# A Strassen-style float32 transformer block: where the first norm's diagonal tiles live, how fast the first FFN's queue drains, and how the projection groups are paired

## The chip, the cores and the metric

The kernel runs on one core of a Trainium2 chip. It is written for the core's engines directly: TensorE (PE in the profile) multiplies, PEld is its weight load, VectorE (DVE) and ScalarE (ACT) work element by element, and SyncE (SP) issues the DMA transfers. The metric is device time in microseconds (us) of one execution, the median over runs.

## The reference

One layer of a streaming encoder on x of shape (1, 1024, 1024), in float32:

```
h = x + 0.5 * SwiGLU_1(RMSNorm(x))                       # w_in 1024 x 5632, w_out 2816 x 1024
u = RMSNorm(h)
q, k, v, g_ret, p, gates = split(u @ w_in)               # 1024 columns each, gates 2048
q, k = rotary(q), rotary(k) / 16                         # 4 heads of 256
ret  = headnorm(retention(q, k, v)) * silu(g_ret)        # chunks of 64, decay per head
pool = (trailing means of p, windows 2/4/8/16, - p) @ pool_w * pool_scale
gate = sigmoid(gates + gate_bias)
h = h + (gate[0] * (ret @ w_ret_up) + gate[1] * (pool @ w_pool_up)) @ w_out
h = h + 0.5 * SwiGLU_2(RMSNorm(h))
return RMSNorm(h)
```

## The kernel before

Everything is float32, made on TensorE from two parts of each operand: a rounded high part, cast by ACT (line 161), and the rest, subtracted by DVE (line 162). A product of two such operands is three matmuls (lines 181 to 183). On top of that each group of 256 output channels by 1024 tokens is computed by a Strassen scheme of seven products (`strassen`): sums of weight blocks (S1 to S4, made by DVE at lines 484 to 501) against sums of input blocks. In a trace `q1a`, `q1b`, `q1e` are the PSUM banks of group q1, `q1ra` and `q1rb` its loaded weight rows, `q1S` a weight sum, `q1wS` and `q1wL` split weights of a sum or a loaded block, and `q1A`, `q1B` the group's two output tiles. An evacuation adds or copies PSUM into such a tile (lines 1200 and 1202 in the projections).

Two groups at a time are interleaved product by product (`pairs` in the projections, `pairs_of_both` in the FFNs), since they share operands; the last two products of a pair share work (`common`), in which the pair's banks `x` and `y` stand.

The order of the work is written in Python and each engine executes it in order. `Flow.run` walks the steps (one per product): it prepares a step's weights four steps ahead, emits the product, and then takes `flow.rate` items from the front of the queue `flow.back`. Into this queue go things that are not urgent: squares and norms, scalings by a norm's row, rotations, windows, gates and stores. `flow.until` (through `mix.rms()` or an operand) pulls items forward until what is asked for is there. All loads and stores go through the one queue of SP, in order (line 140). Tiles come from rings: `raw` and `tl` (128x1024, 4 buffers each; `tl` holds the loaded rows of x at the start), `t4` (128x1024, 9), `c2` (128x512, 8).

RMSNorm is not applied to the inputs. Each token's inverse root is spread over the partitions as a row (`spread`: diagonal tiles times ones on TensorE; n10b and n11b are the two halves for the first norm, n1rb is the row, n2rb that of the second), and outputs that need it are multiplied by that row. In the first FFN (`ffn_in`) a gate tile `ag` is scaled (line 777), put through Silu and multiplied with the up tile (`times`, line 783), and further operand blocks of the first norm (n1x, split into n1R) are made by DVE in the same queue.

The projections handle 24 groups of 256 channels in 12 pairs, in the sequence `order`, each by `project(kind, n)`:

- q and k (n = 0 to 3): not scaled. Groups with n < 3 are rotated here: `rotate` does six DVE operations a half (lines 1221 to 1230), twelve a group; the tables cos and sin are scaled by n2rb first (line 1182). Groups q3 and k3 are turned later, in the retention.
- p (n = 0 to 3): scaled by n2rb, then `window`: n + 1 doublings a half (line 1262) and a mean (lines 1269 to 1272).
- t (n = 0 to 7): the branch gates, scaled by n2rb, then four sigmoids on ACT (line 1249), each stored.
- g (n = 0 to 3): the retention's output gate, scaled, then Silu on ACT (line 1240).

A sigmoid and a Silu each need a table loaded on ACT (ACT_TABLE_LOAD). The scalings, rotations, windows and gates of a group go to the queue, and so run mostly beside the next pair's products.

Of the kernel before, what the change touches and what calls it, by code (L numbers as in the profile page):

```python
# [11 lines left out]
F32R = mybir.dt.float32r  # L12
# [5 lines left out]
P = 128  # L18
S = 1024
D = 1024  # L20
KT = D // P
H = S // 2
# [28 lines left out]
N_MV, N_T4, N_RAW, N_WT, N_TL, N_C2 = 28, 9, 4, 5, 4, 8  # L51
# [39 lines left out]
def block_kernel(ctx: ExitStack, tc, x, x_tok, x_two, vecs, f1_in, f1_out, w_in, w_v, pool_w, w_ret, w_pool, w_o,  # L91
# [8 lines left out]
    flow = Flow()  # L100

    cp = ctx.enter_context(tc.tile_pool(name="cp", bufs=1))
    sb = ctx.enter_context(tc.tile_pool(name="sb", bufs=1))
# [22 lines left out]
    def t4(name):  # L126
        return sb.tile([P, S], F32, tag="t4", bufs=N_T4, name=name)
# [4 lines left out]
    def bank(name):  # L132
        return ps.tile([P, H], F32, tag="ps", name=name)

    def sum_bank(name):

        return ps.tile([P, H], F32, tag="sum", bufs=N_SUM, name=name)
# [4 lines left out]
    def eights(name):  # L142

        return sb.tile([P, 32], F32, tag="ss", bufs=2, name=name)[:, :8]
# [4 lines left out]
    def half(t, j):  # L149
        return t[:, j * H : (j + 1) * H]  # L150
# [9 lines left out]
    def split(hi, lo, src):  # L160
        copy(hi, src)  # L161
        tt(lo, src, hi.bitcast(F32), SUB)  # L162
# [25 lines left out]
    def in_turns(x):  # L188

        return x.rearrange("p (o b a) -> p o a b", b=2, a=4)  # L190

    def in_row(x):
        return x.rearrange("p (o a b) -> p o a b", b=2, a=4)
# [24 lines left out]
    for n in range(N_SUM):  # L218
        b = sum_bank(f"set{n}")
# [7 lines left out]
    def inverse_root(sums, n, name, eps=None):  # L227

        m = sums.shape[-1]

        def st(k):
            return sb.tile([P, 8], F32, tag="st", bufs=10, name=f"{name}{k}")[:, :m]

        v, r0, r1, t = st("v"), st("r0"), st("r1"), st("t")
        for z, e in enumerate(eps or (EPS,)):
            at = slice(z * m // len(eps), (z + 1) * m // len(eps)) if eps else slice(0, m)
            nc.vector.tensor_scalar(v[:, at], sums[:, at], 1.0 / n, e, MUL, ADD)
        act(r0, v, AF.Sqrt)
        nc.vector.reciprocal(r1, r0)

        tt(t, r1, v, MUL)
        stt(t, t, -0.5, r1, MUL, MUL)
        r = sb.tile([P, 8], F32, tag="rt", bufs=3, name=f"{name}r")[:, :m]
        stt(r, t, 1.5, r1, ADD, MUL)
        return r

    def token_sums(ssq, tiles, name):

        sums = bank(f"{name}sum")
        for k, j in enumerate(tiles):  # L250
            mm(sums[:, k : k + 1], ssq[:, j * P : (j + 1) * P], ones[:, :1], start=k == 0, stop=True,
               skip_group_check=True)
        return sums[:, : len(tiles)]

    def spread(r, name):

        n = r.shape[-1]
        b = bank(f"{name}b")[:, : n * P]
        r2 = sb.tile([P, 2, 8], F32R, tag="r2", bufs=1, name=f"{name}r2")
        split(r2[:, 0, :n], r2[:, 1, :n], r)  # L260
        for z in range(2):
            dg = sb.tile([P, H], F32R, tag="c2", bufs=N_C2, name=f"{name}dg{z}")[:, : n * P]
            for j in range(n):
                at, by = dg[:, j * P : (j + 1) * P], r2[:, z, j : j + 1].bitcast(F32)
                if z:
                    nc.vector.tensor_scalar(at, ident, by, None, MUL)
                else:
                    act(at, ident, AF.Copy, scale=by)
            mm(b, ones_r, dg, start=not z, stop=bool(z))
        return b  # L270
# [26 lines left out]
    class Next(Norm):  # L297
# [139 lines left out]
                for i in range(4):  # L437
                    flow.add(lambda f=f, i=i: f(i))

        def stats(self, sums=None, between=()):  # L440
            def roots():
                t = sums if sums is not None else token_sums(self.ssq, range(8), self.name)
                self.r_tok = inverse_root(t, D, self.name)

            def row(q):
                if not q:
                    self.row = t4(f"{self.name}rb")
                to, b = half(self.row, q), spread(self.r_tok[:, 4 * q : 4 * q + 4], f"{self.name}{q}")
                if sums is not None:
                    to, b = in_row(to), in_turns(b)  # L450
                copy(to, b)
                if q:
                    self.rb = self.row

            n = max(0, len(between) - 3)
            flow.add(roots, *between[:n], lambda: row(0), *between[n:], lambda: row(1))
# [656 lines left out]
    first = Next("n1", V_FFN1)  # L1113
# [20 lines left out]
    x_sums = eights("x_sums")  # L1134

    def x_square(t):
        r = tl(f"xs{t}")
        load(r, x_tok[t])
        act(r, r, AF.Square, accum_out=x_sums[:, t : t + 1])

    for t in range(8):
        flow.add(lambda t=t: x_square(t))
    first.stats(x_sums)

    ops1 = spill("r", FH), spill("t", FH), spill("b", FH), spill("m", FH, H)
    h1, h2 = spill("h1", KT), spill("h2", KT)
# [8 lines left out]
    def fetch_rows(w, name):  # L1155
        for k in range(2):
            r = fetched[name, k] = wide(f"{name}ra{k}")
            load(r, w[k, :, :S])

    def ffn1():  # L1160
        for n, step in enumerate(ffn_in(first, f1_in, ops1, "a", lambda: fetch_rows(f1_out, "b"), lead)):
            flow.rate = 1
            yield step
        flow.rate = 2
        yield from ffn_out(first, ops1, ops_done["a"], f1_out, x_two, "b", mix.quarter, end1, fetched)
# [231 lines left out]
        yield from product("L22", "T4", "a", False, result(1, 0))  # L1397

    light = [("t", n) for n in range(8)] + [("g", n) for n in range(4)]
    turned = [(kind, n) for n in range(1, 4) for kind in "qk"]  # L1400
    heavy = [o for pair in zip([("p", n) for n in (1, 3, 2, 0)], turned) for o in pair] + turned[4:]
    order = [("q", 0), ("k", 0), *(o for pair in zip(heavy, light) for o in pair), *light[len(heavy) :]]

    def projections():
        yield from values()
# [472 lines left out]
    class Last(Norm):  # L1878


        tiles, rows, banks, sums = {}, {}, {}, {}
# [68 lines left out]
        def end(self, part):  # L1950
            if part != 3:
                return
            tokens = slice(H, S)
            at = {}

            def stats():
                r = inverse_root(token_sums(self.ssq, range(tokens.start // P, tokens.stop // P), "fin0"), D, "fin0")
                at["b"] = spread(r, "fin0")

            def scale(mt):  # L1960
                t = self.tiles[mt][:, tokens]
                stt(t, t, vec[:, V_FINAL + mt : V_FINAL + mt + 1], at["b"], MUL, MUL)
                load(out[mt, :, tokens], t)

            flow.add(stats, *(lambda mt=mt: scale(mt) for mt in range(KT)))
# [3 lines left out]
    def second():  # L1969
        for n, step in enumerate(ffn_in(ffn2, f2_in, ops2, "c", lambda: fetch_rows(f2_out, "d"))):  # L1970
            flow.rate = 1
            yield step
        flow.rate = 2
    flow.run(chain(ffn1(), projections(), retention(), merge(), second(),
                   ffn_out(ffn2, ops2, ops_done.setdefault("c", set()), f2_out, h2, "d", fin.quarter, fin.end, fetched, fin, f2_far)))
    flow.some(-1)
# [95 lines left out]
```

## Time and profile before

| | us |
|---|---|
| median of 3 runs | 2068.88 |
| the runs | 2070.76, 2068.88, 2068.75 |
| the profiled execution | 2069.82 |
| its span in the trace | 2068.0 |
| first FFN's first gate scaling starts | 84.58 |
| projections' first pair starts | 682.50 |
| retention starts | 1118.74 |

The profiled execution's time contains its span and 1.8 us around it. The granted clock of TensorE is full throughout. In a row of a trace the first number is the start in us from the span's start, the second the duration; `out<-in` are tile names without their buffer numbers; brackets give the engine's idle time before the row and what ended it. A matmul row of 128x512 starts 0.216 us after the one before when nothing is late, although its own duration reads 0.38: the rows overlap in the pipeline. So lost time on TensorE is read from the distances of starts.

### The profile page before, as it was taken

What the parts mean: (1) busy time and instruction counts of PE and PEld (TensorE: products, weight loads), DVE (VectorE), ACT (ScalarE), POOL (GpSimd) and SP (SyncE); (2) the same over time, 40 slices, a digit from 0 to 9 for tenths busy, and PEclk for the clock granted to TensorE, in tenths of its full rate; (3) what the DMA queues carried; (4) which work ended last, traced back from release to release, by engine and by line L of the source; (5) the groups of instructions that cost most, each with busy time, mean ns of one, the idle gap of its engine ahead of it and who ended that gap; (6) DMA issues with size and microseconds to landing.
All of it is one profiled execution on the core that took longest, in us unless ns stands there. A gap on an engine that the chain in (4) does not pass through costs nothing.

```text
span 2068.0 us, 29692 instructions
## 1 busy us (share of the span) xinstructions
PE 2045.2 (99%) x10672; PEld 1810.6 (88%) x10672; DVE 1835.5 (89%) x3262; ACT 1091.5 (53%) x2061; POOL 0.2 (0%) x4
## 2 busy tenths in 40 slices
PE   9999999999999999999999999999999999999998
PEld 7888999988888888888888999888789999998887
DVE  8799998997996798999778888999989989899897
ACT  8545444554653535454447753456645545455454
POOL 0000000000000000000000000000000000000000
PEclk9999999999999999999999999999999999999999
DMA  7232424585543333243336576724223242368642
GB/s 257 88 138 77 143 87 143 199 278 190 186 145 100 115 112 131 85 146 120 122 123 237 189 233 235 253 92 159 75 82 138 88 142 87 133 209 268 215 144 101
DMA packets 118819, 313.57 MB, mean 152 GB/s; under 512 B 13200, under 2 KB 17424, under 8 KB 118672
## 3 DMA queue, kind: packets, MB, share of 16 engines
q1 hardware_dynamic: 118096, 310.64, 44.3%
q8 instruction: 83, 1.36, 0.3%
q10 hardware_dynamic: 576, 1.05, 0.1%
q14 instruction: 64, 0.52, 0.1%
HBM read 220.93 MB, written 90.70 MB: 151 GB/s over the span
## 4 chain that ended last, share of the span: by engine, by line
PE 79%; DVE 14%; ACT 3%; issue 2%; DMA 1%; SPq 0%; ACTq 0%; DVEq 0%
PE a_b L181 2%; PE a_b L182 2%; PE a_b L183 2%; PE c_b L181 2%; PE c_b L182 2%; PE c_b L183 2%; PE a_e L181 2%; PE a_e L183 2%; PE a_e L182 2%; PE c_e L183 2%; PE c_e L182 2%; PE c_e L181 2%; PE a_a L182 1%; PE a_a L181 1%; PE a_a L183 1%
## 5 line engine op out<-in xcount | busy, mean ns | idle before, releaser
L182 PE MATMUL c_b<-n3T,c_wS 128*128 128x512 f32 x176 | 66.8, 380 | 0.0
L181 PE MATMUL c_b<-n3T,c_wS 128*128 128x512 f32 x176 | 66.5, 380 | 0.2 <-ACT n3T L161 0.2
L183 PE MATMUL c_b<-n3T,c_wS 128*128 128x512 f32 x176 | 66.7, 379 | 0.0
L181 PE MATMUL a_b<-n1T,a_wS 128*128 128x512 f32 x168 | 63.7, 379 | 0.0
L182 PE MATMUL a_b<-n1T,a_wS 128*128 128x512 f32 x168 | 63.7, 379 | 0.0
L183 PE MATMUL a_b<-n1T,a_wS 128*128 128x512 f32 x168 | 63.7, 379 | 0.0
L181 PE MATMUL a_a<-n1R,a_wL 128*128 128x512 f32 x120 | 45.5, 379 | 0.0
L183 PE MATMUL a_a<-n1R,a_wL 128*128 128x512 f32 x120 | 45.5, 379 | 0.0
L182 PE MATMUL a_a<-n1R,a_wL 128*128 128x512 f32 x120 | 45.5, 379 | 0.0
L182 PE MATMUL c_a<-n3R,c_wL 128*128 128x512 f32 x112 | 42.7, 381 | 1.1 <-DVE n3R L166 1.1
L181 PE MATMUL c_a<-n3R,c_wL 128*128 128x512 f32 x112 | 42.6, 380 | 0.8 <-ACT c_b L521 0.8
L183 PE MATMUL c_a<-n3R,c_wL 128*128 128x512 f32 x112 | 42.5, 379 | 0.0
L181 PEld LDWEIGHTS c_b<-n3T,c_wS 128*128 128x128 f32 x176 | 33.2, 189 | 5.1 <-ACT n3T L161 0.6
L182 PEld LDWEIGHTS c_b<-n3T,c_wS 128*128 128x128 f32 x176 | 33.3, 189 | 4.8 <-DVE n3T L162 0.3
L183 PEld LDWEIGHTS c_b<-n3T,c_wS 128*128 128x128 f32 x176 | 33.3, 189 | 4.7
L183 PEld LDWEIGHTS a_b<-n1T,a_wS 128*128 128x128 f32 x168 | 31.8, 189 | 4.5
L182 PEld LDWEIGHTS a_b<-n1T,a_wS 128*128 128x128 f32 x168 | 31.8, 189 | 4.4
L181 PEld LDWEIGHTS a_b<-n1T,a_wS 128*128 128x128 f32 x168 | 31.8, 189 | 4.3
L162 DVE TENSOR_TENSOR a_wS<-a_S,a_wS 128x512 fp32r<-128x512 f32 x45 | 30.6, 682 | 5.3 <-ACT a_wS L161 5.2
L161 ACT CAST c_wS<-c_S 128x512 fp32r<-128x512 f32 x46 | 27.8, 622 | 11.8 <-DVE c_S L484 7.4
L182 PE MATMUL c_e<-n3T,c_wL 128*128 128x512 f32 x88 | 33.5, 380 | 0.1
L181 PE MATMUL c_e<-n3T,c_wS 128*128 128x512 f32 x88 | 33.5, 380 | 0.0
(3159 smaller groups left out, 8001.9 us busy)
## 6 DMA issues: line engine op xcount, KB each, us to landing
c_ra<-in_f_in SPq DMA_DIRECT2D x22, 512.0 KB, 3.7
c_rb<-in_f_in SPq DMA_DIRECT2D x22, 512.0 KB, 3.7
a_ra<-in_f_in SPq DMA_DIRECT2D x21, 512.0 KB, 3.8
a_rb<-in_f_in SPq DMA_DIRECT2D x21, 512.0 KB, 3.8
t<-au SPq DMA_DIRECT2D x11, 512.0 KB, 3.0
b<-ag SPq DMA_DIRECT2D x11, 512.0 KB, 3.8
r<-au SPq DMA_DIRECT2D x11, 512.0 KB, 3.7
bra<-in_f_out SPq DMA_DIRECT2D x11, 512.0 KB, 5.3
```

Source lines behind the costliest of these rows:

```text
L161: copy(hi, src)
L162: tt(lo, src, hi.bitcast(F32), SUB)
L181: mm(dst, w[0], m[0], start=start, stop=False, skip_group_check=True)
L182: mm(dst, w[0], m[1], start=False, stop=False, skip_group_check=True)
L183: mm(dst, w[1], m[0], start=False, stop=stop, skip_group_check=True)
```

## The change

Three edits. The first norm's diagonal tiles (`n10dg`, `n11dg`) are halves of one 128x1024 tile from the ring of loaded rows (`tl`), and no longer two tiles from the `c2` ring. While steps 16 to 27 of the first FFN's list run, two items a step are taken off the queue instead of one. And the projections' sequence is another: a gate's group (t) now stands beside each rotated or pooled one from the first pair on.

```diff
--- before.py
+++ after.py
@@ -252,14 +252,19 @@
                skip_group_check=True)
         return sums[:, : len(tiles)]
 
-    def spread(r, name):
+    def spread(r, name, diagonals=None):
 
         n = r.shape[-1]
         b = bank(f"{name}b")[:, : n * P]
         r2 = sb.tile([P, 2, 8], F32R, tag="r2", bufs=1, name=f"{name}r2")
         split(r2[:, 0, :n], r2[:, 1, :n], r)
+        if diagonals:
+            wide_dg = sb.tile([P, S], F32R, tag=diagonals[0], bufs=diagonals[1], name=f"{name}dg")
         for z in range(2):
-            dg = sb.tile([P, H], F32R, tag="c2", bufs=N_C2, name=f"{name}dg{z}")[:, : n * P]
+            if diagonals:
+                dg = half(wide_dg, z)[:, : n * P]
+            else:
+                dg = sb.tile([P, H], F32R, tag="c2", bufs=N_C2, name=f"{name}dg{z}")[:, : n * P]
             for j in range(n):
                 at, by = dg[:, j * P : (j + 1) * P], r2[:, z, j : j + 1].bitcast(F32)
                 if z:
@@ -437,7 +442,7 @@
                 for i in range(4):
                     flow.add(lambda f=f, i=i: f(i))
 
-        def stats(self, sums=None, between=()):
+        def stats(self, sums=None, between=(), diagonals=None):
             def roots():
                 t = sums if sums is not None else token_sums(self.ssq, range(8), self.name)
                 self.r_tok = inverse_root(t, D, self.name)
@@ -445,7 +450,7 @@
             def row(q):
                 if not q:
                     self.row = t4(f"{self.name}rb")
-                to, b = half(self.row, q), spread(self.r_tok[:, 4 * q : 4 * q + 4], f"{self.name}{q}")
+                to, b = half(self.row, q), spread(self.r_tok[:, 4 * q : 4 * q + 4], f"{self.name}{q}", diagonals)
                 if sums is not None:
                     to, b = in_row(to), in_turns(b)
                 copy(to, b)
@@ -1140,7 +1145,7 @@
 
     for t in range(8):
         flow.add(lambda t=t: x_square(t))
-    first.stats(x_sums)
+    first.stats(x_sums, diagonals=("tl", N_TL))
 
     ops1 = spill("r", FH), spill("t", FH), spill("b", FH), spill("m", FH, H)
     h1, h2 = spill("h1", KT), spill("h2", KT)
@@ -1159,7 +1164,7 @@
 
     def ffn1():
         for n, step in enumerate(ffn_in(first, f1_in, ops1, "a", lambda: fetch_rows(f1_out, "b"), lead)):
-            flow.rate = 1
+            flow.rate = 2 if 16 <= n < 28 else 1
             yield step
         flow.rate = 2
         yield from ffn_out(first, ops1, ops_done["a"], f1_out, x_two, "b", mix.quarter, end1, fetched)
@@ -1397,9 +1402,9 @@
         yield from product("L22", "T4", "a", False, result(1, 0))
 
     light = [("t", n) for n in range(8)] + [("g", n) for n in range(4)]
-    turned = [(kind, n) for n in range(1, 4) for kind in "qk"]
-    heavy = [o for pair in zip([("p", n) for n in (1, 3, 2, 0)], turned) for o in pair] + turned[4:]
-    order = [("q", 0), ("k", 0), *(o for pair in zip(heavy, light) for o in pair), *light[len(heavy) :]]
+    turned = [(kind, n) for n in range(3) for kind in "qk"]
+    heavy = [o for pair in zip(turned, [("p", n) for n in (1, 3, 2, 0)]) for o in pair] + turned[4:]
+    order = [*(o for pair in zip(heavy, light) for o in pair), ("q", 3), ("k", 3), *light[len(heavy) :]]
 
     def projections():
         yield from values()
```

The pairs in order, before and after:

```
before  (q0,k0) (p1,t0) (q1,t1) (p3,t2) (k1,t3) (p2,t4) (q2,t5) (p0,t6) (k2,t7) (q3,g0) (k3,g1) (g2,g3)
after   (q0,t0) (p1,t1) (k0,t2) (p3,t3) (q1,t4) (p2,t5) (k1,t6) (p0,t7) (q2,g0) (k2,g1) (q3,k3) (g2,g3)
```

Instructions move at the start of the first FFN and in the projections up to the start of the retention; elsewhere each engine's sequence is the same. Line numbers behind the first edit are five higher in the changed file.

On TensorE, in the first FFN: `a_e`, `a_b` and `a_a` are banks of its first groups, `n1R` and `n1T` the input blocks. Before, the first half of the norm's row stands here:

```order
L182 MATMUL a_e<-n1T_754,a_wL_847 128x512
L183 MATMUL a_e<-n1T_754,a_wL_847 128x512
L269 MATMUL n10b<-n10dg_966,ones_r 128x512
L269 MATMUL n10b<-n10dg_972,ones_r 128x512
L181 MATMUL a_b<-n1R_446,a_wS_869 128x512
L182 MATMUL a_b<-n1R_446,a_wS_869 128x512
```

After, it stands six products earlier:

```order
L182 MATMUL a_b<-n1R_464,a_wS_724 128x512
L183 MATMUL a_b<-n1R_464,a_wS_724 128x512
L274 MATMUL n10b<-n10dg,ones_r 128x512 x2
L181 MATMUL a_a<-n1R_310,a_wL_751 128x512
L182 MATMUL a_a<-n1R_310,a_wL_751 128x512
```

The second half (n11b) moves by the same distance.

On VectorE, in the second pair of the projections (p1 with its gate group), where the last sums of weights are made. Before, k0's rotation stands between them:

```order
L162 TENSOR_TENSOR t0wS_7082<-t0S_7080,t0wS_7082 128x512
L501 TENSOR_TENSOR p1S_7036<-p1ra,p1S_7036 128x512
L162 TENSOR_TENSOR p1wS_7102<-p1S_7011,p1wS_7102 128x512
L1221 TENSOR_TENSOR k0b_7120<-k0B,sin 128x512
L1222 TENSOR_TENSOR k0c_7121<-k0A,sin 128x512
L501 TENSOR_TENSOR t0S_7080<-t0ra,t0S_7080 128x512
L162 TENSOR_TENSOR t0wS_7125<-t0S_7058,t0wS_7125 128x512
L1225 TENSOR_TENSOR k0A<-k0A,cos 128x512
```

After, with t1 in t0's place:

```order
L502 TENSOR_TENSOR t1rb<-t1ra,t1rb 128x512
L1234 TENSOR_TENSOR q0B<-q0B,cos 128x512
L489 TENSOR_TENSOR t1S_7081<-t1S_7059,t1ra 128x512
L162 TENSOR_TENSOR t1wS_7062<-t1rb,t1wS_7062 128x512
L1235 TENSOR_TENSOR q0B<-q0B,q0c_7034 128x512
L506 TENSOR_TENSOR p1S_7037<-p1ra,p1S_7037 128x512
L162 TENSOR_TENSOR t1wS_7083<-t1S_7081,t1wS_7083 128x512
L162 TENSOR_TENSOR p1wS_7103<-p1S_7012,p1wS_7103 128x512
```

k0's twelve operations are in the fourth pair now; two scalings of t0 (line 1212) stand at the head of this pair instead.

On ScalarE, in the same pair, before (p1p and p1v are copies of p1's banks):

```order
L161 CAST t0wS_7061<-t0rb 128x512
L543 COPY p1p_7118<-p1e 128x512
L161 CAST t0wS_7082<-t0S_7080 128x512
L161 CAST p1wS_7102<-p1S_7011 128x512
L161 CAST t0wS_7125<-t0S_7058 128x512
```

And after:

```order
L161 CAST t1wS_7062<-t1rb 128x512
L548 COPY p1p_7119<-p1e 128x512
L1254 ACT_TABLE_LOAD
L1254 ACTIVATE t0z_7121<-t0A,vec 128x512
L161 CAST t1wS_7083<-t1S_7081 128x512
L161 CAST p1wS_7103<-p1S_7012 128x512
L1254 ACTIVATE t0z_7124<-t0A,vec 128x512
L531 COPY p1v<-p1b 128x512
```

The sigmoids of t0 and the load of their table come forward from the third pair into the second.

## The prediction

> **What bounds the kernel now.** I read the busy line first, then the waits of TensorE (PE), then the starts of the work's stages on PE, and last the engines in the stretches around the two places that the change touches.
>
> ```profile
> PE 2045.2 (99%) x10672; PEld 1810.6 (88%) x10672; DVE 1835.5 (89%) x3262; ACT 1091.5 (53%) x2061; POOL 0.2 (0%) x4
> ```
>
> PE carries 99% of the span and no matmul is removed, so nothing can be gained but the time in which PE waits. The waits of PE that lie in the two places are these (engine, line, what released it: us in total, times, longest):
>
> ```profile
> PE a_y L181 <- ACT n1R L161: 1.0, 1, 1.0
> PE k1b L181 <- DVE k1B L1200: 0.6, 1, 0.6
> PE q1b L181 <- ACT q1v L526: 0.5, 1, 0.5
> PE g2a L181 <- ACT g2b L521: 0.5, 1, 0.5
> PE t1e L183 <- DVE t1wS L162: 0.5, 1, 0.5
> PE t1e L181 <- ACT t1wS L161: 0.5, 1, 0.5
> PE t0e L183 <- DVE t0wL L162: 0.3, 1, 0.3
> PE q1e L183 <- DVE q1wS L162: 0.2, 1, 0.2
> ```
>
> A wait also costs some tenths as the pipeline refills, which this list leaves out. The full price is read from starts. In the projections each pair of groups begins with one product's first matmul; these are the starts of pairs 1 to 6 and 12 of the old order, and of the retention behind them:
>
> ```profile
> 682.50 0.38 PE L181 MATMUL q0a<-n2R,q0wL 128*128 128x512 f32 x1
> 719.50 0.38 PE L181 MATMUL p1a<-n2R,p1wL 128*128 128x512 f32 x1
> 755.80 0.38 PE L181 MATMUL q1a<-n2R,q1wL 128*128 128x512 f32 x1
> 795.13 0.38 PE L181 MATMUL p3a<-n2R,p3wL 128*128 128x512 f32 x1
> 830.90 0.38 PE L181 MATMUL k1a<-n2R,k1wL 128*128 128x512 f32 x1
> 867.60 0.38 PE L181 MATMUL p2a<-n2R,p2wL 128*128 128x512 f32 x1
> 1082.22 0.38 PE L181 MATMUL g2a<-n2R,g2wL 128*128 128x512 f32 x1
> 1118.74 0.28 PE L181 MATMUL s<-q,k 128*128 128x256 f32 x1
> ```
>
> Pairs 6 to 11 take 214.62 us, 35.77 each, and pair 4 (795.13 to 830.90) takes 35.77 too: that is a pair in which PE never waits. Against it pair 2 (719.50 to 755.80) is 0.53 longer, pair 3 (to 795.13) 3.56, pair 5 (to 867.60) 0.93, pair 12 0.75. Why these, the stretches tell (us; then PE, PEld, DVE, ACT, POOL busy, clock, DMA share, GB/s):
>
> ```profile
> 60.00:84.60 24.60, 24.60 (x116) 21.47 (x115) 14.22 (x30) 12.38 (x28) 0.00 (x0) 1.00 0.14 43
> 84.60:111.40 26.80, 25.86 (x123) 22.56 (x121) 26.73 (x43) 14.49 (x23) 0.00 (x0) 1.00 0.50 180
> 713.50:753.50 40.00, 39.78 (x211) 35.26 (x209) 39.93 (x69) 14.61 (x27) 0.00 (x0) 1.00 0.30 102
> 753.50:783.50 30.00, 28.20 (x123) 22.67 (x124) 26.86 (x45) 15.46 (x31) 0.00 (x0) 1.00 0.40 136
> 859.50:1082.00 222.50, 222.50 (x1165) 198.77 (x1166) 189.10 (x321) 106.01 (x196) 0.00 (x0) 1.00 0.36 125
> ```
>
> VectorE (DVE) is full without a gap in 84.6 to 111.4 and in 713.5 to 753.5, and in both cases PE's waits come right behind: DVE runs late, and what it feeds arrives late. In 60 to 84.6 it idles 10 us. From 859.5 on it has 33 us to spare and PE loses nothing.
>
> **The change part by part.** *The first norm's row.* In the first FFN the row that scales the gates by each token's norm is made by four matmuls, and the first gate scaling waits for it:
>
> ```profile
> 64.67 0.38 PE L181 MATMUL a_a<-n1R,a_wL 128*128 128x512 f32 x1
> 80.21 0.63 PE L269 MATMUL n10b<-n10dg,ones_r 128*128 128x512 f32 x2
> 84.58 1.23 DVE L777 TENSOR_TENSOR ag<-ag,n1rb 128x1024 f32<-128x1024 f32 x1 [1.40 <-ACT n1rb L451]
> 110.19 0.28 PE L183 MATMUL a_x<-n1R,a_wx 128*128 128x256 f32 x1
> 111.48 0.38 PE L181 MATMUL a_y<-n1R,a_ws 128*128 128x256 f32 x1 [1.02 <-ACT n1R L161]
> 123.47 0.38 PE L181 MATMUL a_a<-n1R,a_wL 128*128 128x512 f32 x1
> ```
>
> The order puts n10b's two matmuls, now at 80.21, ahead of the product that begins at 64.67: 15.5 us earlier, and n11b's likewise. The number of matmuls, diagonal tiles and copies stays, so nothing is paid for that. The scalings (1.2 us each), multiplies and new operand blocks that pile up from 84.58 on then start in the stretch with 10 us of idle DVE. The wait before a_y is 111.48 - 110.19 less a normal step of 0.11, 1.18; with it twelve delays from 111.48 to 123.47 come to 2.2. I take -1.8 (the first four, 1.6, and half of the small ones), with the ends 0 (the operand block, not the row, was what came late) and -2.2. The diagonals in the rows' ring take one of four buffers for a while; loads of the next rows behind it have 15 us to recover, since the stretch moves 43 GB/s at a DMA share of 0.14: 0.
>
> *Pair 1, now q0 with t0.* A gate group has to be scaled by the second norm's row, k0 had not. So one scaling now stands ahead of the second half's diagonals, for which PE waits already:
>
> ```profile
> 703.08 0.67 DVE L266 TENSOR_SCALAR n21dg<-cst,n21r 128x128 fp32r<-128x128 f32 x3
> 703.67 0.73 PE L269 MATMUL n21b<-n21dg,ones_r 128*128 128x512 f32 x2
> ```
>
> A DVE operation of 128x512 advances the queue by 0.60 (the rotation rows below give it). Nothing is between, so PE waits up to that much longer: +0.45, ends 0 (DVE waits for ACT there anyway) and +0.7.
>
> *Pair 2, p1 with t1 instead of t0.* Before, DVE rotates q0 and k0 in this stretch; the second half of k0 alone is these, the first and the last of twelve rows:
>
> ```profile
> 736.96 0.68 DVE L1221 TENSOR_TENSOR k0b<-k0B,sin 128x512 f32<-128x512 f32 x1
> 751.61 0.68 DVE L1230 TENSOR_TENSOR k0B<-k0B,k0c 128x512 f32<-128x512 f32 x1
> ```
>
> Twelve rotations of k0 at 0.60 are 7.2 us of DVE, moved out to pair 4, where q1's stood. Two scalings of t0 (1.2) come in at the head, and two k0 row sums come forward. DVE ends the pair 4 to 5 us less late, so the 0.53 at t0wL goes: -0.53 (ends 0 and -0.53). But ScalarE (ACT) now does t0's sigmoids here, with the table they need, where before they stood in pair 3:
>
> ```profile
> 773.30 1.28 ACT L1249 ACT_TABLE_LOAD   x1
> 774.59 0.84 ACT L1249 ACTIVATE t0z<-t0A,vec 128x512 f32<-128x512 f32 x1
> 734.11 0.62 ACT L161 CAST t0wS<-t0S 128x512 fp32r<-128x512 f32 x1
> 737.63 0.38 PE L181 MATMUL t0b<-n2T,t0wS 128*128 128x512 f32 x1
> ```
>
> The cast of the partner's second sum ended at 734.73 and was used at 737.63, 2.9 to spare. Load and one sigmoid now stand ahead of it (1.29, and some 0.75 until the next starts: 2.0), and the split on DVE follows it (0.60). That leaves 0.3, and the two scalings ahead of it on DVE (1.2) can eat that: +0.3, ends 0 and +0.9.
>
> The Trainium skill, page "ScalarE: Activation LUTs", section "What ACT_TABLE_LOAD costs", says a switch of tables is about 1283 ns of load and another 1380 ns of drain. The load agrees with the 1.28 above, but the drain does not show: the first sigmoid starts 1.29 after the load's start. Were it paid here, the cast would come 1.38 later, the term be 1.7 and not 0.3, and the time 2064.8.
>
> *Pair 3, k0 with t2 instead of q1 with t1.* DVE comes into it 4 to 5 us earlier, and finds p1's windows as before. The best guide is the old order itself: new pairs 2 and 3 stand as old pairs 4 and 5 did (a pooled group after a rotated one, then a rotated one), and those cost 0 and 0.93 more than undisturbed. The 0.93 (k1b, in the list of waits) came where p3's windows, four doublings a half by the code, held up k1B on DVE; p1 has two. So I take 0.3 left of 3.56: -3.3, ends -2.6 (0.93 left) and -3.56.
>
> *Pairs 4 to 8* keep their order operation by operation, each with the next gate: 0, with -0.93 as an end should k1b's wait go. *Pairs 9 to 11:* k2's rotation moves and q3 and k3 pair with each other; the 33 us of idle DVE from 859.5 on cover it: 0. Without that cover the twelve rotations would show.
>
> *Pair 12* is (g2,g3) in both, but the pair ahead was (k3,g1) and is (q3,k3), which has no Silu. Now g1's stand ahead of the copy for which PE waits:
>
> ```profile
> 1086.45 1.06 ACT L1240 ACTIVATE g1B<-g1B 128x1024 f32<-128x1024 f32 x1 [0.68 <-DVE g1B L1207]
> ```
>
> With both Silus and their scalings gone, ACT is free for the copy: -0.75, ends 0 and -0.75. The gates g0 and g1 are stored earlier, with no one late for it.
>
> The sum: -1.8 + 0.45 - 0.53 + 0.3 - 3.3 - 0.75 = -5.6. The profiled execution took 2069.82 with a span of 2068.0, 0.94 above the median of 2068.88; the sum is taken off the median, as the waits are the same few in every execution: 2063.3. All lower ends together are -2.2 - 0.53 - 3.56 - 0.93 - 0.75 = -8.0, 2060.9; all upper ends +0.7 + 0.9 - 2.6 = -1.0, 2067.9.
>
> **The rivals.** *One place alone pays.* DVE's arrears are carried and not paid off: pair 2 still has q0's twelve rotations with both table scalings ahead, and its new sigmoids and scalings delay t1wS and through it everything of pair 3. For it: DVE is full over 40 us there. Against: it loses 7.2 of work and gets 1.2. If 2.5 of pair 3's 3.56 stay, the sum is -3.1 and the time 2065.8, within 0.2% (4.1 us, about what a measurement of this kernel can tell from no change). The mirror case, in which the first FFN gives nothing because the row was not the cause, gives -3.8 and 2065.1, no change to be told either.
>
> *The drain is paid* and the sum is 2064.8, as above.
>
> *Slower: the load queue.* SP issues loads and stores in order. In the new order the load of k0's second rows stands behind the stores of all four t0 sigmoids, as k1's stood behind t1's in old pair 4:
>
> ```profile
> 815.43 0.38 SPq L140 DMA_DIRECT2D k1rb<-in_w_in  x1
> DMA to landing us min/median/max: 4.7/4.7/4.7
> 820.51 0.69 DVE L484 TENSOR_TENSOR k1S<-k1rb 128x512 f32<-128x512 f32 x1
> ```
>
> It landed at 820.13 and DVE took it at 820.51: 0.4 of slack, at 25.4 after the pair's start. In new pair 2 the sigmoids come 1.3 later for the table, but DVE also comes later, by two scalings of the tables (1.2 each) that pair 4 has not, so some 1.5 of slack remain. If the sigmoids slip further, DVE stops with t1's evacuation and weight splits behind it, and PE one step later, us for us. To end slower by over 4.1 it would have to cancel -5.6 and add that, a landing 11 us late; on the wrong side of zero from 7 us on. At 7 us late: 2070.3; at 11: 2073.0. Only a store that waits for a late sigmoid could do it.
>
> **How the numbers follow.** Forecast as summed: 0.58. One place alone (either): 0.30. Drain: 0.06. Queue: 0.04, and 0.02 for what I do not see. The forecast lies below 2064.7 (faster by over 0.2%) in nine tenths of its range, 0.53; three tenths of the one-place case do (0.09: pair 5's 0.93 gained beside it), and the unseen 0.02: faster 0.64. Same is the rest of these and the drain, 0.05 + 0.21 + 0.06 = 0.32; slower 0.04. The likeliest case's own range is 2061.3 to 2065.2. The range to hold 8 in 10 takes in the one-place case and stops short of the queue's: 2060.9 to 2067.2.
>
> **What would show it.** Right, if n1rb's scaling starts near 69, no wait stands at a_y, pairs 2 and 3 start 36.1 and 36.1 apart, and pair 12 takes 35.8. The pair 1 term is right if the matmuls of n21b wait some 0.45 longer. The list of PE's waits should keep k1b's place with another name (q1b against p3's windows). Wrong, if t1wS or a k0 load heads the waits of pair 2 with more than 1 us, if the first FFN's operand blocks are late with the row early, or if the retention's first stage, which follows pair 12, waits for what q3 and k3 store later.

## The result and the profile after

| us | before | after |
|---|---|---|
| median (22 runs each) | 2069.61 | 2066.26 |
| lowest to highest | 2067.26 to 2071.32 | 2064.99 to 2069.48 |
| the profiled execution | 2069.82 | 2065.11 |
| its span | 2068.0 | 2063.2 |

The ratio is 0.9984 with a 95% interval of 0.9978 to 0.9990: 3.4 us less, 0.16%. It is a small gain that is clear of no change, and just below the 0.2% that the prediction drew as its bound; 2066.3 lies in the range of 2060.9 to 2067.2, 3 us above the predicted 2063.3, and above the 2061.3 to 2065.2 that the prediction gave its likeliest case.

These rows of the changed kernel answer to those of before. The starts of pairs 1 to 6 and 12 of the new order, and of the retention:

```profile
680.14 0.38 PE L181 MATMUL q0a<-n2R,q0wL 128*128 128x512 f32 x1
717.35 0.38 PE L181 MATMUL p1a<-n2R,p1wL 128*128 128x512 f32 x1
754.95 0.38 PE L181 MATMUL k0a<-n2R,k0wL 128*128 128x512 f32 x1
790.72 0.38 PE L181 MATMUL p3a<-n2R,p3wL 128*128 128x512 f32 x1
826.49 0.38 PE L181 MATMUL q1a<-n2R,q1wL 128*128 128x512 f32 x1
863.18 0.38 PE L181 MATMUL p2a<-n2R,p2wL 128*128 128x512 f32 x1
1077.80 0.38 PE L181 MATMUL g2a<-n2R,g2wL 128*128 128x512 f32 x1
1113.57 0.28 PE L181 MATMUL s<-q,k 128*128 128x256 f32 x1
```

Pair 1 takes 37.21 (37.00 before), pair 2 37.60 (36.30), pair 3 35.77 (39.33), pair 5 36.69 (36.70), pair 12 35.77 (36.52). The loss of pair 3 is gone to the last tenth, and pair 2 has become the worst. Its waits, and the others in the places of the change, in the list of TensorE's waits:

```profile
PE t1b L181 <- ACT t1v L531: 1.0, 1, 1.0
PE q1b L181 <- DVE q1B L1205: 0.6, 1, 0.6
PE s L181 <- ACT k L161: 0.5, 1, 0.5
PE a_y L181 <- ACT n1R L161: 0.4, 1, 0.4
```

The engines in the stretches (the projections' ones moved with the start of pair 1):

```profile
60.00:84.60 24.60, 24.60 (x116) 21.48 (x115) 21.99 (x40) 16.30 (x31) 0.00 (x0) 1.00 0.24 86
84.60:111.40 26.80, 26.80 (x135) 23.71 (x134) 22.40 (x42) 11.19 (x22) 0.00 (x0) 1.00 0.46 156
711.30:751.10 39.80, 38.66 (x198) 33.61 (x197) 37.82 (x64) 18.04 (x32) 0.00 (x0) 1.00 0.37 122
751.10:781.00 29.90, 29.90 (x147) 26.36 (x146) 25.14 (x41) 15.16 (x30) 0.00 (x0) 1.00 0.32 113
```

In 60 to 84.6 VectorE works 22.0 us and not 14.2, and in the next stretch it is full no longer. In the first FFN the row's scaling and the operand block stand so:

```profile
64.42 0.62 PE L274 MATMUL n10b<-n10dg,ones_r 128*128 128x512 f32 x2
68.83 1.23 DVE L782 TENSOR_TENSOR ag<-ag,n1rb 128x1024 f32<-128x1024 f32 x1 [1.52 <-ACT n1rb L456]
104.15 0.69 DVE L403 TENSOR_TENSOR n1x<-n1R 128x512 f32<-128x512 f32 x1
114.33 0.38 PE L181 MATMUL a_y<-n1R,a_ws 128*128 128x256 f32 x1 [0.39 <-ACT n1R L161]
```

The row came 15.8 us earlier, as worked out. The first operand block came 4.0 us earlier; before, it stood here:

```profile
108.17 0.68 DVE L398 TENSOR_TENSOR n1x<-n1R 128x512 f32<-128x512 f32 x1
```

The wait before a_y shrank and did not vanish. Added up over the starts from 60 to 130 us, TensorE loses 0.94 and not 2.21. In what follows "lost" always means such a sum: distances of starts over those of an undisturbed neighbour.

In pair 2 ScalarE does this (its rows from the table's load on, those named here):

```profile
732.94 1.28 ACT L1254 ACT_TABLE_LOAD   x1
734.23 0.84 ACT L1254 ACTIVATE t0z<-t0A,vec 128x512 f32<-128x512 f32 x1
...
738.99 0.84 ACT L1254 ACTIVATE t0z<-t0B,vec 128x512 f32<-128x512 f32 x1
...
740.86 0.58 ACT L548 COPY t1p<-t1e 128x512 f32<-128x512 f32 x1
...
741.86 0.59 ACT L531 COPY t1v<-t1b 128x512 f32<-128x512 f32 x1
```

TensorE then begins its next product on that bank:

```profile
742.50 0.48 PE L181 MATMUL t1b<-n2T,t1wS 128*128 128x512 f32 x1 [1.01 <-ACT t1v L531]
```

Between 733 and 740 ScalarE has to do the load, four sigmoids and the casts that pair 2 needs; the copy t1v, which frees bank t1b, comes at the end of all that. By the starts this costs TensorE 1.27: 1.17 at the wait and 0.10 at the matmul behind it.

The rest of the 1.83 us that pair 2 loses are smaller pieces. 0.15 stand at the first matmuls of t1b, on the sum that is cast behind the load and the first sigmoid. 0.39 stand at t1e, on the sum before it, whose cast and split are these:

```profile
731.83 0.62 ACT L161 CAST t1wS<-t1rb 128x512 fp32r<-128x512 f32 x1 [2.98 <-DVE t1rb L502]
732.86 0.70 DVE L162 TENSOR_TENSOR t1wS<-t1rb,t1wS 128x512 fp32r<-128x512 f32 x1
```

This cast stands ahead of the load, so these 0.39 are not ScalarE's. VectorE comes to the split 15.51 us after the pair's start; before, it came to the same split 14.45 us after it:

```profile
733.95 0.68 DVE L162 TENSOR_TENSOR t0wS<-t0rb,t0wS 128x512 fp32r<-128x512 f32 x1
```

The difference of the two traces by places, in us: first FFN -1.27, pair 1 +0.21, pair 2 +1.30, pair 3 -3.56, pair 5 -0.01, pair 12 -0.75, together -4.1. The remaining -0.7 of the spans lies where the order is the same in both kernels (the start, the second norm, the retention) and differs from one execution to the next.

### The profile page after: what moved, and what is told of

It is laid out like the page before. It is cut to its first block, busy times and chain, and to the rows that moved or that the text cites. A ratio compares the mean times of both kernels' runs of the same rounds, so it can differ in the third digit from the quotient of the medians.

```text
span 2063.2 us, 29713 instructions
## 1 busy us (share of the span) xinstructions
PE 2042.8 (99%) x10672; PEld 1810.5 (88%) x10672; DVE 1836.2 (89%) x3263; ACT 1090.9 (53%) x2060; POOL 0.2 (0%) x4
## 4 chain that ended last, share of the span: by engine, by line
PE 83%; DVE 11%; ACT 2%; issue 2%; DMA 1%; SPq 0%; ACTq 0%; DVEq 0%
PE c_b L181 2%; PE c_b L182 2%; PE c_b L183 2%; PE a_b L181 2%; PE a_b L183 2%; PE a_b L182 2%; PE c_e L183 2%; PE c_e L182 2%; PE c_e L181 2%; PE a_e L183 2%; PE a_e L181 2%; PE a_e L182 2%; PE a_a L183 1%; PE a_a L181 1%; PE a_a L182 1%
## 5 line engine op out<-in xcount | busy, mean ns | idle before, releaser
L162 DVE TENSOR_TENSOR c_wS<-c_S,c_wS 128x512 fp32r<-128x512 f32 x46 | 31.9, 696 | 2.4 <-ACT c_wS L161 2.3
L161 ACT CAST a_wS<-a_S 128x512 fp32r<-128x512 f32 x45 | 27.4, 621 | 12.2 <-PE a_a L183 6.1
```

## The experiments

Each comparison is with runs of the kernel before on the same chip, whose medians lay between 2068.8 and 2069.8. A ratio can differ by up to 0.0005, about 1 us, from the quotient of the two medians beside it, so smaller differences are read from the traces and not from the times.

**One part at a time.** `ffn_part` is the changed kernel with the old order of the projections, `order_part` the kernel before with the new one.

```diff
 # ffn_part, against the changed kernel
-    turned = [(kind, n) for n in range(3) for kind in "qk"]
...
+    turned = [(kind, n) for n in range(1, 4) for kind in "qk"]
...
```

> The kernel before with the first FFN's two edits (diagonals in the loaded rows' ring, two items a step for steps 16 to 27) and the old order of the projections. Theory (the two places are independent, and in the first FFN the row came late): TensorE loses 0.9 to 1.0 us between 60 and 130 us instead of 2.2, the projections keep pair 3 at 39.3 and pair 12 at 36.5; time 1.2 us below before (0.8 to 1.6). Rival (the first FFN's edits gain nothing, the row was not the cause): 0 within 0.5 us, and an a_y wait of about 1 us stays. Second rival (the retention's new 0.7 us wait for ACT's cast of k near 1231 comes from this part): it shows here.

> The kernel before with the new order of the projections alone. Theory (VectorE's arrears at pair 3 are paid off, part comes back in pair 2 through ScalarE's sigmoids): pair 3 35.8 instead of 39.3, pair 12 35.8 instead of 36.5, pairs 1 and 2 together 74.8 instead of 73.3; the first FFN keeps its 2.2 us lost; time 2.8 us below before, or 2.1 if the retention's new wait (0.7 us) belongs to the order. Rival (pair 2's new wait at t1v comes from the first FFN's edit, which shifts the transfers): pairs 1 and 2 take 73.5 and the time is 4.1 below before.

`ffn_part` took 2067.52 against 2068.81, ratio 0.9994 (0.9985 to 1.0003); TensorE lost 0.94 between 60 and 130, and pair 3 kept 39.32. `order_part` took 2067.03 against the same, 0.9994 (0.9985 to 1.0002); it lost 2.21 in the first FFN, pair 3 took 35.77, pairs 1 and 2 together 74.64. By time neither is clear of no change alone; by the traces each does its part whatever the other does, and the wait at t1v belongs to the order:

```profile
PE a_y L181 <- ACT n1R L161: 1.0, 1, 1.0
PE t1b L181 <- ACT t1v L526: 0.9, 1, 0.9
```

(both from `order_part`). The first point where the expectations fell: pair 12 of `ffn_part` took 35.77, with the old order and g1's Silus ahead. More on that below. The rival by which pair 2's wait came from shifted transfers has fallen.

**The two edits of the first FFN.** `rate_alone` has only the faster queue, `diag_alone` only the diagonals' other ring, both with the old order.

```diff
 # rate_alone, against before (in ffn1)
-            flow.rate = 1
+            flow.rate = 2 if 16 <= n < 28 else 1
```

> The kernel before with two items a step for steps 16 to 27 of the first FFN, the diagonals left in the c2 ring, old order of the projections. Theory A (the faster queue moves the row by itself, the ring of the diagonals does not matter): n10b near 64.7, TensorE loses 0.9 to 1.0 between 60 and 130, time 1.2 us below before, as with both edits. Theory B (four of eight c2 buffers held by diagonals hold up the weight sums that take theirs from the same ring): new waits of TensorE of 1 to 3 us between 60 and 80, time at or above before.

> The kernel before with the diagonals in the loaded rows' ring alone, one item a step, old order. Theory (the ring neither moves the row nor frees anything that is waited for): TensorE loses 2.2 between 60 and 130 as before, time within 0.5 us of before; pair 3 39.3. Rival (the ring gives the c2 tiles back to the weight sums): 0.5 us or more less lost between 60 and 130.

`rate_alone` took 2067.45 against 2068.81, ratio 0.9998 (0.9989 to 1.0007), and lost 0.95 in the first FFN, the same as with both edits. The first half of the row stood here:

```profile
64.51 0.63 PE L269 MATMUL n10b<-n10dg,ones_r 128*128 128x512 f32 x2
```

In `diag_alone` (2069.05 against 2069.39, 0.9998, 0.9989 to 1.0007) it stood where it did before, and 2.20 were lost:

```profile
80.04 0.63 PE L274 MATMUL n10b<-n10dg,ones_r 128*128 128x512 f32 x2
```

So the rate moves the row and earns the 1.3 us that the traces show, too little for these intervals to tell by time; the ring of the diagonals moves nothing and costs nothing. Theory B (diagonals in c2 hold up the weight sums) has fallen: no new wait showed between 60 and 80.

**Why pair 3 was late.** Two things left pair 3 at once in the change: VectorE's arrears from k0's rotation, and the load of the sigmoid's table. `no_k0_turn` takes the first away (it leaves k0 unturned), `old_order_table_early` the second, each in the kernel before.

```diff
 # no_k0_turn, against before (in project)
-                turn = (*rotate(0), *rotate(1)) if n < NH - 1 else ()
+                turn = (*rotate(0), *rotate(1)) if n < NH - 1 and (kind, n) != ("k", 0) else ()
 # old_order_table_early, against before (in rotate)
                 if not tab:
                     rotary_tables()
+                    act(warm, tab["sin"][:, S - 1 :], AF.Sigmoid)
```

> The kernel before with the rotation of k0 left out (twelve operations of VectorE, 7.2 us, in pair 2); k0 is stored unturned, the rest is unchanged, its sigmoids and their table load still stand in pair 3. Theory A (pair 3 is late because VectorE is): pair 3 takes 36.3 or less instead of 39.3, pair 2 35.8. Theory B (pair 3 is late because the table is loaded in it): pair 3 stays at 38 or more.

> The kernel before with the sigmoid's table loaded at the start of pair 2 (one more sigmoid of one column) and no longer in pair 3. Theory A (VectorE's arrears make pair 3 late, the load only adds to the last of the waits): pair 3 falls by at most 0.7 from 39.3. Theory B (the load is the cause): it falls by 1.3 or more.

In `no_k0_turn` pairs 2 and 3 begin and end here:

```profile
718.56 0.38 PE L181 MATMUL p1a<-n2R,p1wL 128*128 128x512 f32 x1
754.33 0.38 PE L181 MATMUL q1a<-n2R,q1wL 128*128 128x512 f32 x1
790.10 0.38 PE L181 MATMUL p3a<-n2R,p3wL 128*128 128x512 f32 x1
```

35.77 each, undisturbed, with the load and t0's sigmoids still in pair 3. In `old_order_table_early` pair 3 runs between these:

```profile
755.80 0.38 PE L181 MATMUL q1a<-n2R,q1wL 128*128 128x512 f32 x1
793.92 0.38 PE L181 MATMUL p3a<-n2R,p3wL 128*128 128x512 f32 x1
```

38.12, 1.2 less than 39.33: more than theory A allowed (0.7), a little less than theory B asked (1.3). The arrears are the cause, since without them nothing is left; with them, the load adds 1.2. Their single executions took 2064.12 and 2068.99.

**Why pair 2 is late now.** `table_early` is the changed kernel with the same early sigmoid.

> The changed kernel with one more ScalarE instruction: a sigmoid of one column of the scaled sin table, so that the sigmoid's table is loaded at the start of pair 2 and not in its middle. Theory A (the table load of 1.28 us is what makes t1wS and t1v late in pair 2): pairs 1 and 2 take 73.6 instead of 74.8, time 1.2 us below the changed kernel. Theory B (the four sigmoids, some 3 us of ScalarE in a stretch in which it also casts, are enough by themselves): the waits at t1v keep at least 0.9 and the time is within 0.4 of the changed kernel. Theory C (the page's drain of 1.38 beside the load is hidden in the wait too): pairs 1 and 2 fall to 73.3 and the first sigmoid starts at once.

It took 2064.69 against 2068.81, 0.9982 (0.9973 to 0.9990). Its first two pairs take 73.87 and not 74.81, between these starts:

```profile
680.37 0.38 PE L181 MATMUL q0a<-n2R,q0wL 128*128 128x512 f32 x1
754.24 0.38 PE L181 MATMUL k0a<-n2R,k0wL 128*128 128x512 f32 x1
```

The load stands where ScalarE has time, and none precedes the first sigmoid:

```profile
716.09 1.28 ACT L1223 ACT_TABLE_LOAD   x1
733.23 0.84 ACT L1255 ACTIVATE t0z<-t0A,vec 128x512 f32<-128x512 f32 x1
```

In the list of TensorE's waits only this is left in pair 2, the one at t1v is gone:

```profile
PE t1e L183 <- DVE t1wS L162: 0.2, 1, 0.2
```

Theory A holds, with 0.94 for the expected 1.2: what is lost at t1v falls from 1.27 to 0.33 by the starts, and ScalarE now stands idle for 1.22 ahead of that copy, waiting for VectorE, so the four sigmoids alone don't hold it up. The loss at t1e stays (0.41), as it must if it is VectorE's. Four other traces with the new order and the load in its old place have 74.64 to 74.92 for the two pairs, and the other two with the early load 73.83 and 73.71, so the gain is no accident of one execution. Theory C (a drain on top) gets no support: in the changed kernel the copy before the load ends at 732.93, the load starts at 732.94 and the first sigmoid 1.29 later.

**What is left of a_y's wait.** `rate_longer` keeps two items a step up to step 39.

```diff
-            flow.rate = 2 if 16 <= n < 28 else 1
+            flow.rate = 2 if 16 <= n < 40 else 1
```

> The changed kernel with two items a step up to step 39 of the first FFN and not 27. Theory A (what is left of a_y's wait, 0.55, is the queue's length: the new operand blocks n1x stand behind the gates' work): the wait goes, TensorE loses 0.4 or less between 60 and 130, time 0.5 below the changed kernel. Theory B (the faster queue puts gate work ahead of weight sums of the next steps): new waits of 0.5 to 2 and a time equal to or above the changed kernel.

2064.98 against 2069.79, 0.9977 (0.9968 to 0.9986). Nothing at all is lost between 60 and 130. The operand blocks begin at 99.3, where they began at 104.2 in the changed kernel and at 108.2 before:

```profile
99.33 1.29 DVE L403 TENSOR_TENSOR n1x<-n1R 128x512 f32<-128x512 f32 x2
```

Theory A holds: the rest of the wait was the queue's length too. TensorE's gain is 0.94, where 0.5 was expected.

**Pair 5, the wait that the change left alone.** `edge_on_dve` moves the short edge copies of the windows from ScalarE to VectorE; `p3_with_q3` changes the sequence, so that p3's windows meet no sigmoids.

```diff
 # edge_on_dve, against the changed kernel (in window)
-                copy(o[:, :step], s[:, :step])
+                nc.vector.tensor_scalar(o[:, :step], s[:, :step], 1.0, None, MUL)
 # p3_with_q3, against the changed kernel
-    order = [*(o for pair in zip(heavy, light) for o in pair), ("q", 3), ("k", 3), *light[len(heavy) :]]
+    order = [(s[0], int(s[1])) for s in "q0 t0 p1 t1 k0 t2 q1 t3 p2 t4 k1 t5 p0 t6 q2 t7 p3 q3 k2 g0 k3 g1 g2 g3".split()]
```

> The changed kernel with the short edge copies of the pooling windows on VectorE and not on ScalarE, so that the doublings no longer go to and fro between two queues. Theory A (pair 5's 0.93 is a doubling that waits for an edge copy behind sigmoids): pair 5 35.8 instead of 36.7, time 0.9 below the changed kernel. Theory B (VectorE is late by its own load there): pair 5 stays at 36.7 or more, time equal.

> The changed kernel with another sequence of pairs: (q0,t0) (p1,t1) (k0,t2) (q1,t3) (p2,t4) (k1,t5) (p0,t6) (q2,t7) (p3,q3) (k2,g0) (k3,g1) (g2,g3). p3's windows now run beside no sigmoids, and pair 12 has g1's Silus ahead again, as before the change. Theory A (the 0.93 is p3's doublings, held up by tiles that sigmoids still read): no pair of the first eleven but 1 and 2 takes more than 35.8. Theory B (it is VectorE's load by p3 alone): the pair behind p3 still takes 36.4 or more. For pair 12: if Silus ahead of the copy cost 0.75 by themselves it takes 36.5; if they only cost it when the last rows land late, 35.8.

`edge_on_dve` took 2067.08 against 2069.79, 0.9989 (0.9980 to 0.9998): pair 5 still 36.77, and 0.56 more in pair 7. Theory A has fallen. What held VectorE is in its rows ahead of q1B (of `edge_on_dve`; the changed kernel has the same wait, 0.78):

```profile
850.45 1.22 DVE L1267 TENSOR_TENSOR p3s<-p3s 128x1022 f32<-128x1022 f32 x1 [0.77 <-ACT t3z L1254]
...
854.83 0.68 DVE L1205 TENSOR_TENSOR q1B<-q1b,q1p 128x512 f32<-128x512 f32 x1
```

The doubling of p3 waits for t3's sigmoids (the new tile takes the place of one that they read), and then three doublings stand in a row ahead of the evacuation. `p3_with_q3` bears it out: pairs 3 to 8 take 35.77, pair 9 (p3 itself) 36.03 and pair 10, with p3's windows and no sigmoids, 35.77. Time 2065.43 against 2069.39, 0.9980 (0.9971 to 0.9989). With q3 beside p3 VectorE is also spared the scalings of a gate group, but `p3_late`, below, keeps such scalings (those of g1) beside p3's windows, without sigmoids, and its next pair takes 35.77 as well. That it is the ring of tiles, and not another tie between windows and sigmoids, was not tried by itself.

**Pair 12.** g1's Silus stand ahead of the copy g2b in seven kernels (before, the five others with the old order, and `p3_with_q3`). Pair 12 took 36.4 to 36.5 in four of their traces (before, `rate_alone`, `old_order_table_early`, `p3_with_q3`) and 35.77 in three. What tells them apart is whether VectorE had to wait for g3's last rows to land. In `ffn_part`, with 35.77, it had not:

```profile
1078.35 0.69 DVE L489 TENSOR_TENSOR g3S<-g3rb 128x512 f32<-128x512 f32 x1
```

In `p3_with_q3`, with 36.46, it had:

```profile
1076.78 0.69 DVE L489 TENSOR_TENSOR g3S<-g3rb 128x512 f32<-128x512 f32 x1 [1.30 <-DMA g3rb<-in_w_in]
```

And in the changed kernel they were late too, as in `order_part` (1.35) and `edge_on_dve` (1.01), with pair 12 undisturbed in all three:

```profile
1076.61 0.69 DVE L489 TENSOR_TENSOR g3S<-g3rb 128x512 f32<-128x512 f32 x1 [1.20 <-DMA g3rb<-in_w_in]
```

So by these traces it takes both, the Silus and the late rows; the change removes one of them, and gains 0.7 in some executions only. The lateness of the rows was observed, not set.

**Together.** `early_and_longer` joins the early table and the longer queue; `p3_late` adds a sequence in which p3 stands late beside g1.

```diff
 # p3_late, against early_and_longer
+    order = [(s[0], int(s[1])) for s in "q0 t0 p1 t1 k0 t2 q1 t3 p2 t4 k1 t5 p0 t6 q2 t7 k2 g0 p3 g1 q3 k3 g2 g3".split()]
```

> The changed kernel with both gains of the earlier runs: the sigmoid's table loaded at the start of pair 2 and two items a step up to step 39. Theory (they stand in different places and add up): TensorE loses 0.1 or less between 60 and 130, pairs 1 and 2 take 73.9, time 1.9 us below the changed kernel, 5.2 below before. Rival (the first FFN's faster queue only shifts the wait to the second norm or to the retention): time 1.0 below the changed kernel.

> The kernel with the early table and the longer faster queue, and with the sequence (q0,t0) (p1,t1) (k0,t2) (q1,t3) (p2,t4) (k1,t5) (p0,t6) (q2,t7) (k2,g0) (p3,g1) (q3,k3) (g2,g3): p3's windows run beside g1's Silu and no sigmoids, and no Silu stands ahead in pair 12. Theory (p3's doublings cost only beside sigmoids): every pair from the third on takes 35.8, 0.9 less than with the two gains alone, time 2.8 us below the changed kernel, 6.1 below before. Rival (pairs 10 and 11 hold k2's rotation and p3's windows one behind the other and VectorE falls behind there): 0.5 to 2 us more in pair 11, time no better than with the two gains.

`early_and_longer` took 2064.18 against 2069.39, 0.9973 (0.9962 to 0.9983); nothing lost in the first FFN, 73.83 in pairs 1 and 2: the two add up. `p3_late` took 2062.77 against 2069.62, 0.9972 (0.9960 to 0.9984): every pair from the third on takes 35.77.

```profile
752.76 0.38 PE L181 MATMUL k0a<-n2R,k0wL 128*128 128x512 f32 x1
1074.69 0.38 PE L181 MATMUL g2a<-n2R,g2wL 128*128 128x512 f32 x1
1110.46 0.28 PE L181 MATMUL s<-q,k 128*128 128x256 f32 x1
```

From 752.76 to 1110.46 are ten times 35.77. Of the 5.8 us that pairs 2 to 12 lost before (0.53 + 3.56 + 0.93 + 0.75), 0.7 are left, all in pair 2. By its interval it beats before and, at 0.9972 against 0.9984, probably the changed kernel, with which it was not run side by side. The gains over the changed kernel of `table_early` (0.9982), `rate_longer` (0.9977) and `early_and_longer` (0.9973), and that of `p3_late` over the last of these, are too small for such intervals; they are shown by the traces alone.

## Why the prediction was right, and where it was not

- *The first FFN*: forecast -1.8, measured -1.27. The mechanism held in its outline (row 15.8 us earlier, VectorE's work in its idle stretch). The size failed at counting the whole a_y wait as the row's: 0.55 of it was the queue still being too slow, which `rate_longer` showed. The term's end of 0 had named this cause, the operand block and not the row coming late. No run moves the row and leaves the rest of the queue where it was, so what the row earns by itself stays open. The diagonals' ring at 0: right.
- *Pair 1*: forecast +0.45, measured +0.21. The scaling made the diagonals 0.29 later after the pair's start (20.87 and not 20.58), and not 0.60. Part of it went into idle time that VectorE had ahead of them (0.42 before, 0.24 now), the lower end's reason; the rest was not traced.
- *Pair 2*: forecast -0.53 + 0.3 = -0.23, measured +1.30, outside the term's own ends of -0.53 and +0.9. This is the step that failed. Its gain at t0wL came. Its price was worked out for one consumer, the second cast, against the load and one sigmoid, and there 0.15 was lost for the 0.3. One sum earlier, where the forecast had no term, 0.39 were lost at t1e, probably to the two scalings at the head of the pair (1.2 of VectorE, against the 1.06 by which the split came later). Above all, everything behind the four sigmoids on ScalarE's queue moves too, and the copy t1v, the last of it, was not looked at. It cost 1.27. Following ScalarE to the end of what was inserted would have put that copy in question: 1.28 + 4 x 0.75 of new work in the 9 us from 732.9 to 741.9.
- *Pair 3*: forecast -3.3, measured -3.56, and the cause was the stated one (`no_k0_turn`). The comparison with old pairs 4 and 5 gave bounds that hold the result, at their best end.
- *Pairs 4 to 11*: 0, as forecast; pair 5 kept its 0.9 with q1b in k1b's place, as said. That p3's windows were its cause is borne out; the link to them, tiles that sigmoids hold, it had not.
- *Pair 12*: -0.75 in the profiled executions, as forecast, but with late rows as a second condition that the forecast had in its trace (DVE's wait for g3rb) and did not price as a chance. Over the seven kernels with the Silus ahead the mean is 0.4.
- *The rivals*: "one place alone pays" named the mechanism that came, new sigmoids in pair 2, but sent it into pair 3, which stayed free. The load queue did not bind, but it was closer than thought: k0's second rows landed some 0.3 before VectorE took them at 744.40, where the forecast left 1.5. The drain did not show: the Trainium skill, page "ScalarE: Activation LUTs", section "What ACT_TABLE_LOAD costs", gives 1283 ns for the load, which agrees with 1.28 here, and about 1380 ns of drain, for which there is no room in the 1.29 from the load's start to the first sigmoid's.
- *The total*: with pair 12 at its mean the places give -1.27 + 0.21 + 1.30 - 3.56 - 0.41 = -3.7, against -3.4 measured (interval -4.6 to -2.1). The forecast of -5.6 was 1.5 too good in pair 2 and 0.5 in the first FFN. "Faster by over 0.2%" had the larger chance; the measured 0.16% falls on the other side of that bound. That the range still held is owed to its width: it was drawn to take in a case in which pair 3 keeps 2.5 us, and what came instead were shortfalls of 1.5 in pair 2 and of 0.5 in the first FFN. The 0.2% was also taken for about the least that can be told from no change; the interval of 0.9978 to 0.9990 tells 0.16%.
- *The signs*: n1rb's scaling started at 68.83 (near 69 was said), pair 12 took 35.77, and q1b took k1b's place in the list of waits, all as said. But a_y still waited, pairs 2 and 3 took 37.60 and 35.77 where 36.1 each was said, and the loss at n21b's matmuls grew by 0.08 and not by 0.45. The operand blocks were late with the row early, which the prediction had named as a sign of being wrong.
- *Its sums*: the first four delays and half of the rest make 1.9, not 1.8. 2063.3 and 1.38 of drain make 2064.7, not 2064.8. A load 7 us late against 1.5 of slack loses 5.5 and ends at 2068.8, not 2070.3. The two rows given for the second half of k0's rotation are the first and the last of both halves. Only the first of these touches the forecast, by 0.1.

## What to carry to other kernels

When work is inserted into an in-order queue, follow every instruction behind it to the queue's next idle gap, and not only the one with the least slack in sight: the last of them paid here. A function table can be loaded where the engine idles, by one tiny use of the function; by the traces that was worth 0.9 us for one line. And if two engines' arrears meet in one stretch, take each away alone before naming the cause: without the arrears of VectorE the load cost nothing, with them 1.2.

## What the runs showed of the hardware

The same transfer lands at different times in executions of the same order. In nine of the fourteen traces, with either order, TensorE waited 0.2 to 0.8 at s in the retention, each time after ScalarE had waited for the load of pu5raw. In a tenth trace that load was late too, by less, and no wait is listed. In before it had not:

```profile
1229.83 0.62 ACT L161 CAST pu5w<-pu5raw 128x512 fp32r<-128x512 f32 x1 [5.34 <-PE ob L182]
```

In the changed kernel it had, 0.8 us by the starts that the change has no part in (old orders have the wait too, and `order_part` has it not):

```profile
1225.51 0.62 ACT L161 CAST pu5w<-pu5raw 128x512 fp32r<-128x512 f32 x1 [6.21 <-DMA pu5raw<-in_w_pool]
```

So a difference of one us between two single executions tells little, even where a trace names its place; the same place in a dozen traces does.
